# Contiguous decay rows, two wide operations on them, and modulation rows 2 to 5 formed on VectorE in the merge

## The chip, the cores and the metric

The kernel runs on one core of a Trainium2 chip. The metric is the device time of one execution in microseconds. The core has TensorE (PE, with a separate view for its weight loads, PEld), VectorE (DVE), ScalarE (ACT), GpSimd (POOL) and SyncE (SP); SP issues nearly all DMAs, in its program's order.

## The reference, cut to what matters

One layer: a token mixer with three branches (S5, Mamba-2, gated linear recurrence) that are merged by gates, then an expert-choice MoE. Both halves are modulated by six rows of 1024 values, `sc @ w_mod + b_mod`. Rows 0 and 1 are needed at the start; rows 2 to 5 only behind the merge. In the Mamba-2 branch the 1024 positions are cut in 8 chunks of 128. In a chunk each of 16 heads has a 128x128 matrix of decays, the exponential of a difference of running sums, for the forward and for the backward direction.

```python
def _mamba2_branch(z, xbc, dt_raw, p, h0):
    ...
    for d in range(2):
        dtd = dtv[:, :, d]
        xs, la, bs, cs = xm * dtd[..., None], dtd * a[d], bm, cm
        if d == 1:
            xs, la, bs, cs = _rev(xs), _rev(la), _rev(bs), _rev(cs)
        yd, fin = _ssd_scan(xs, la, bs, cs, None if h0 is None else h0[d])
        y = y + (yd if d == 0 else _rev(yd))

def _ssd_scan(xs, la, bm, cm, h0):           # chunks of 128 steps
    ...
    cb = jnp.einsum('bcqgn,bcsgn->bgcqs', cm, bm)
    lmat = jnp.exp(_segsum(a))
    y_diag = jnp.einsum('bgjcqs,bcsgjp->bcqgjp', cb[:, :, None] * lmat, xs)
    ...
    decay_out = jnp.exp(a_cum).transpose(0, 3, 4, 1, 2)
    y_off = jnp.einsum('bcqgn,bcgjpn->bcqgjp', cm, entering) * decay_out[..., None]

def _token_mixer(h, p, h0, rows):
    ...
    merged = g[:, :, 0] * ya + g[:, :, 1] * yb + g[:, :, 2] * yc
    return merged @ p['w_o'], (sa, sb, sc)

mod_x = jnp.split((sc @ w_mod[i] + b_mod[i])[:, None, :], 6, axis=-1)
mx, _ = _token_mixer(_modulate(x, norm1_g[i], mod_x[0], mod_x[1]), p, ctx_states, rows)
x = x + mod_x[2] * mx
x = x + mod_x[5] * _expert_choice_moe(_modulate(x, norm2_g[i], mod_x[3], mod_x[4]), p)
```

## The kernel before, in words

Everything is float32; large products are split in a high and a low part and made of three matmuls (L265, L266, L267). The stages follow one another in the span: modulation rows 0 and 1 and the norm; the projections and S5 (to about 530 us); the Mamba-2 stage, called p2 in the code (to 1131); the first half of the merge (1131 to 1270), its second half (to 1355), the output projection and router (to 1535), the experts.

In p2 the rows of running sums `XA` are transposed and stored to the DRAM tile `rowsd` by two DMAs (L731). `states()` then runs 9 steps in which POOL forms `xd` (L750), PE the state sums `st` (L752) and DVE scales the running state (`Sn`, L756). `chunk(g, c)` follows for 4 groups of heads and 8 chunks. It loads `xe`, `bc` and `rowb`: the last is 2 directions x 4 heads x 128 values, the same on all 128 partitions (L793), with three buffers. ACT forms `dec` from it (L796). DVE takes a column of `XL` off each of the 8 pieces of 128x128 and takes the smaller of that and `lim` (L801). ACT takes the exponential of all (L802), POOL adds the two directions (L803), DVE multiplies by `pcb` (L804), the product B times C from PE (L798). POOL multiplies `dec` by C (L805). PE then forms `yps` from `rowb` and `dec` (L814, L815). Every fourth chunk, `xq` is finished and stored to `m2_dram`.

Between the chunks stand other tasks: `z_task` (pj_z), the recurrence `lru_tile` (lps, lr, li, lq), `gate_task` (24 projections, pj_gt, ACT evacuates them as `gz` at L779) and `mod_task`, which for each half of modulation rows 2 to 5 loads 16 pieces `wm` of 128x1024 (two buffers, L909) and multiplies each on PE with a single column `scc`, so that the sums over 8 pieces stand in one bank `pm` (L912). Then the bias row `mr` is loaded, added (L917) and stored to `modd` (L918).

Nothing here is ordered by hand: a scheduler sets the order of each engine and of SP by its own estimate of times, and the pools decide which buffer is waited for. Evacuations have a higher priority. The output projection and the experts are ordered by hand and are not touched.

In the first half of the merge a loop over 8 output tiles d takes a load of weights (`raw_s`, split in `whi_s` and `wlo_s`, L972 and L973), and for each half of 512 positions three products of 12 matmuls: bog, bov and bol. ACT and DVE evacuate them (L1029 to L1033) into `mgs`, stored to `mgd`. At the end of a tile `load_y` loads one tile of `m2_dram` as `yr_m`, scales it (L985) and splits it in the pair `ym[d]` (L993, L994) for the second half of the merge. Modulation row 2 is read behind the merge, the others later.

## Time and profile before

| | us |
|---|---|
| median of three runs | 2121.89 (2120.39 to 2122.43) |
| the profiled execution | 2120.92 |
| its span in the trace | 2119.1 |
| PE busy | 1919.3 |
| DVE busy | 1525.2 |
| ACT busy | 1020.3 |
| POOL busy | 510.4 |

The span is what the trace shows of the profiled execution; 1.8 us lie around it. Busy times are of the whole span and mix stages with different limits. Matmuls overlap in the pipeline, so the durations of single matmuls add up to more than PE's busy time. PEclk is the share of full speed that TensorE's clock was granted.

### The profile page before, as it was taken

What the parts mean: (1) busy time and instruction counts of PE and PEld (TensorE: products, weight loads), DVE (VectorE), ACT (ScalarE), POOL (GpSimd) and SP (SyncE); (2) the same over time, 40 slices, a digit from 0 to 9 for tenths busy, and PEclk for the clock granted to TensorE, in tenths of its full rate; (3) what the DMA queues carried; (4) which work ended last, traced back from release to release, by engine and by line L of the source; (5) the groups of instructions that cost most, each with busy time, mean ns of one, the idle gap of its engine ahead of it and who ended that gap; (6) DMA issues with size and microseconds to landing.
All of it is one profiled execution on the core that took longest, in us unless ns stands there. A gap on an engine that the chain in (4) does not pass through costs nothing.

```text
span 2119.1 us, 27213 instructions
## 1 busy us (share of the span) xinstructions
PE 1919.3 (91%) x9630; PEld 1516.2 (72%) x9630; DVE 1525.2 (72%) x2232; ACT 1020.3 (48%) x1313; POOL 510.4 (24%) x489
## 2 busy tenths in 40 slices
PE   5989999988889988879999999898299999999997
PEld 2678888877657666456577888687188888888885
DVE  4787788783454777667434655628899999999998
ACT  4434434432213665446332212222188888888785
POOL 1353333330142344233100000234501111100122
PEclk9999999999999999989999999999599999999999
DMA  8234334422586676777666554554599999999983
GB/s 313 54 81 114 101 95 117 122 90 90 180 261 192 186 212 175 242 180 210 208 174 188 180 160 153 186 200 149 196 339 381 400 389 404 387 389 393 391 312 137
DMA packets 301554, 462.67 MB, mean 218 GB/s; under 512 B 39945, under 2 KB 200121, under 8 KB 300393
## 3 DMA queue, kind: packets, MB, share of 16 engines
q1 hardware_dynamic: 297096, 445.19, 62.2%
q0 software_dynamic: 4320, 15.73, 2.9%
q8 instruction: 76, 1.25, 0.2%
q14 instruction: 62, 0.50, 0.1%
HBM read 384.44 MB, written 78.51 MB: 218 GB/s over the span
## 4 chain that ended last, share of the span: by engine, by line
PE 55%; DMA 9%; DVE 7%; issue 2%; ACT 1%; SPq 1%; POOL 1%; DVEq 0%; ACTq 0%; POOLq 0%
PE h_w L1443 6%; PE h_w L1445 6%; PE h_w L1444 6%; PE wo L1268 3%; DMA rowb<-rowsd 3%; PE py_w L1445 3%; PE py_w L1443 3%; PE py_w L1444 3%; PE pj_gt L267 2%; PE pj_gt L265 2%; PE pj_gt L266 2%; DMA wm<-in_w_mod_dram 2%; PE bom L266 1%; PE bom L265 1%; PE st L752 1%
## 5 line engine op out<-in xcount | busy, mean ns | idle before, releaser
L1338 DVE TENSOR_TENSOR el_w<-er_w,eh_w 128x1024 fp32r<-128x1024 f32 x384 | 460.7, 1220 | 25.0 <-ACT eh_w L1337 11.1
L1337 ACT CAST eh_w<-er_w 128x1024 fp32r<-128x1024 f32 x384 | 403.7, 1052 | 135.4 <-PE h_w L1444 58.9
L1443 PE MATMUL h_w<-eh_w,thi_x 128*128 128x512 f32 x512 | 202.9, 396 | 0.0
L1445 PE MATMUL h_w<-el_w,thi_x 128*128 128x512 f32 x512 | 200.2, 391 | 0.0
L1444 PE MATMUL h_w<-eh_w,tlo_x 128*128 128x512 f32 x512 | 199.8, 390 | 0.0
L801 DVE SCALAR_TENSOR_TENSOR rowb<-rowb,XL,lim 128x128 f32<-128x128 f32 x256 | 116.1, 518 | 72.1 <-ACT dec L796 72.1
L265 PE MATMUL pj_gt<-hxh,whi_gt 128*128 128x512 f32 x384 | 155.9, 406 | 11.9 <-ACT gz L779 11.9
L267 PE MATMUL pj_gt<-hxh,wlo_gt 128*128 128x512 f32 x384 | 155.3, 404 | 0.0
L266 PE MATMUL pj_gt<-hxl,whi_gt 128*128 128x512 f32 x384 | 155.1, 404 | 0.0
L1445 PEld LDWEIGHTS h_w<-el_w,thi_x 128*128 128x128 f32 x512 | 96.2, 188 | 20.4
L1444 PEld LDWEIGHTS h_w<-eh_w,tlo_x 128*128 128x128 f32 x512 | 96.5, 188 | 19.6 <-DVE tlo_x L1362 0.4
L1443 PEld LDWEIGHTS h_w<-eh_w,thi_x 128*128 128x128 f32 x512 | 96.5, 188 | 19.2 <-ACT thi_x L1361 0.2
L265 PEld LDWEIGHTS pj_gt<-hxh,whi_gt 128*128 128x128 f32 x384 | 74.4, 194 | 38.0 <-ACT gz L779 16.1
L1346 POOL DMA_INDIRECT xs<-h2d,idx x16 | 23.3, 1459 | 309.5 <-PE tb_x L1354 294.4
L1443 PE MATMUL py_w<-eh_w,thi_h 128*128 128x512 f32 x240 | 96.3, 401 | 0.0
L1445 PE MATMUL py_w<-el_w,thi_h 128*128 128x512 f32 x240 | 94.0, 392 | 0.0
L1444 PE MATMUL py_w<-eh_w,tlo_h 128*128 128x512 f32 x240 | 93.5, 390 | 0.0
L267 PEld LDWEIGHTS pj_gt<-hxh,wlo_gt 128*128 128x128 f32 x384 | 74.4, 194 | 25.4 <-issue 9.6
L266 PEld LDWEIGHTS pj_gt<-hxl,whi_gt 128*128 128x128 f32 x384 | 74.4, 194 | 20.5 <-issue 4.9
L796 ACT ACTIVATE dec<-rowb 64x512 f32<-64x512 f32 x64 | 40.2, 629 | 82.7 <-DMA rowb<-rowsd 72.7
L267 PE MATMUL pj_xb<-hxh,wlo_xb 128*128 128x512 f32 x192 | 76.8, 400 | 0.5 <-DVE wlo_xb L128 0.5
L265 PE MATMUL pj_xb<-hxh,whi_xb 128*128 128x512 f32 x192 | 76.7, 399 | 0.0
(653 smaller groups left out, 4894.7 us busy)
## 6 DMA issues: line engine op xcount, KB each, us to landing
er_w<-in_moe_w_dram SPq DMA_DIRECT2D x384, 512.0 KB
wm<-in_w_mod_dram SPq DMA_DIRECT2D x32, 512.0 KB
rowb<-rowsd SPq DMA_DIRECT2D x32, 512.0 KB
raw_gt<-in_w_in_dram SPq DMA_DIRECT2D x24, 512.0 KB
gtd<-gz SPq DMA_DIRECT2D x48, 256.0 KB
xk<-xed SPq DMA_DIRECT2D x18, 512.0 KB
wm<-in_w_mod_dram SPq DMA_DIRECT2D x8, 1024.0 KB
xe<-xed SPq DMA_DIRECT2D x32, 256.0 KB
```

What stands on the lines that cost most here:

```text
L265: T.matmul(ps, wh(k), xh(k), start=(first and k == 0), stop=False)
L266: T.matmul(ps, wh(k), xl(k), start=False, stop=False)
L267: T.matmul(ps, wl(k), xh(k), start=False, stop=(last and k == nk - 1))
L796: A.activation(dec[64 * d:64 * d + 64], rowb[64 * d:64 * d + 64, d], AF.Exp)
L801: V.scalar_tensor_tensor(rowb[:, d, h], rowb[:, d, h], XL[:, c, d, 4 * g + h:4 * g + h + 1], lim[:, d], op0=ALU.subtract, op1=ALU.min)
L1268: T.matmul(st4[i]["ps"][n], ms[i][a][:, k], wo[k][b][:, sl], start=(k == 0 and q == 0), stop=(k == KC - 1 and q == 2))
L1337: A.copy(a, raw)
L1338: V.tensor_sub(b, raw, a.bitcast(F32))
L1346: G.indirect_dma_start(out=xsb[e], out_offset=None, in_=h2d[:, :], in_offset=bass.IndirectOffsetOnAxis(ap=idx[:, e:e + 1], axis=0))
L1443: T.matmul(ps[n], xa[:, j, :], a[:, sl], start=(j == 0), stop=False)
L1444: T.matmul(ps[n], xb[:, j, :], a[:, sl], start=False, stop=False)
L1445: T.matmul(ps[n], xa[:, j, :], b[:, sl], start=False, stop=(j == KC - 1))
```

## The change

Three things. (1) `rowsd` is laid out by group, chunk, direction, head and position. The stores become eight DMAs instead of two, and the load of `rowb` takes one run of 4 KB for each partition, where it was eight runs of 512 bytes. (2) The eight small DVE operations of a chunk become two over 128x1024 with broadcast operands: a subtraction (L801 after) and a minimum (L802). The sum of the two directions is on DVE (L804) instead of POOL. (3) `mod_task` is gone from p2. `mod_part(q, j)` loads one piece `wm` in the first half of the merge and multiplies it on DVE by `scc`, as a value for each partition, adding to the sum of row q (L1001 for the first piece, L1003 for the seven others). When 8 pieces are summed, two matmuls with a column of ones add the partitions (L1008). 5, 5, 5, 5, 4, 4, 4 and 0 pieces follow the store of output tiles 0 to 7. The pieces share 16 buffers with the pairs `ym[d]`, which are now taken one tile at a time.

```diff
--- before.py
+++ after.py
@@ -676,7 +676,7 @@
     lru_dram = dr.tile([4, P, S], F32, name="lru_dram")
     modd = dr.tile([4, D], F32, name="modd")
     m2_dram = [dr.tile([P, 2, S], F32, name=f"m2_dram{g}") for g in range(4)]
-    rowsd = dr.tile([4, 2, 4, S], F32, name="rowsd")
+    rowsd = dr.tile([4, 8, 2, 4, P], F32, name="rowsd")
     rbd = dr.tile([1, S], F32, name="rbd")
     gtd = [[dr.tile([P, S], F32, name=f"gtd{b}{d}") for d in range(KC)] for b in range(3)]
     zp = hstack.enter_context(tc.tile_pool(name="zp", bufs=1, reuse_waits="tile"))
@@ -728,7 +728,8 @@
                 T.transpose(pr_[0:32, q * P:(q + 1) * P], XA[:, 4 * h + q].rearrange("p d h -> p (d h)"), ident)
             V.tensor_copy(rw[:, h * 512:(h + 1) * 512], pr_[0:32, :])
         for d in range(2):
-            Y.dma_start(dap(rowsd, d * 4 * S, [[8 * S, 4], [S, 4], [1, S]]), rw[16 * d:16 * d + 16])
+            for g in range(4):
+                Y.dma_start(dap(rowsd, g * 8 * S + d * 512, [[P, 4], [8 * P, 8], [1, P]]), rw[16 * d + 4 * g:16 * d + 4 * g + 4].rearrange("h (c q) -> h c q", c=8))
         Dc = p2.tile([P, 8], F32, name="Dc")
         for hh in range(2):
             Y.dma_start(Dc[64 * hh:64 * hh + 64, :], dap(I["m2_d"], hh, [[0, 64], [2, 8]]))
@@ -790,17 +791,17 @@
             Y.dma_start(bc_, bcd[g][:, :, q0:q0 + P])
             Bc, Cd = bc_[0:64, 0, :], bc_[:, 1, :]
             rowb = p2.tile([P, 2, 4, P], F32, tag="rowb", name=f"rowb{g}{c}", bufs=3)
-            Y.dma_start(rowb.rearrange("p d h q -> p (d h) q"), dap(rowsd, g * 8 * S + q0, [[0, P], [S, 8], [1, P]]))
+            Y.dma_start(rowb.rearrange("p d h q -> p (d h q)"), dap(rowsd, (8 * g + c) * 8 * P, [[0, P], [1, 8 * P]]))
             dec = p2.tile([P, 4, P], F32, tag="dec", name=f"dec{g}{c}", bufs=2)
             for d in range(2):
                 A.activation(dec[64 * d:64 * d + 64], rowb[64 * d:64 * d + 64, d], AF.Exp)
             pcb = bank(f"pcb{g}{c}")
             T.matmul(pcb[:, 0:P], Bc, Cd[0:64, :], start=True, stop=True)
-            for d in range(2):
-                for h in range(4):
-                    V.scalar_tensor_tensor(rowb[:, d, h], rowb[:, d, h], XL[:, c, d, 4 * g + h:4 * g + h + 1], lim[:, d], op0=ALU.subtract, op1=ALU.min)
+            sh = [P, 2, 4, P]
+            V.tensor_sub(rowb, rowb, XL[:, c, :, 4 * g:4 * g + 4][:, :, :, None].to_broadcast(sh))
+            V.tensor_tensor(rowb, rowb, lim[:, :, None, :].to_broadcast(sh), op=ALU.min)
             A.activation(rowb, rowb, AF.Exp)
-            G.tensor_add(rowb[:, 0], rowb[:, 0], rowb[:, 1])
+            V.tensor_add(rowb[:, 0], rowb[:, 0], rowb[:, 1])
             V.tensor_mul(rowb[:, 0], rowb[:, 0], pcb[:, None, 0:P].to_broadcast([P, 4, P]))
             G.tensor_mul(dec, dec, Cd[:, None, :].to_broadcast([P, 4, P]))
             if c % 4 == 0:
@@ -900,23 +901,6 @@
                     Y.dma_start(lru_dram[t], hs)
                 yield
 
-
-        def mod_task(half):
-            pm = psp.tile([P, 512], F32, tag="pm", name=f"pm2_{half}", bufs=1)
-            for j in range(KC):
-                for q in range(2):
-                    wm = p2.tile([P, 1024], F32, tag="wm2", name=f"wm{half}{j}{q}", bufs=2)
-                    Y.dma_start(wm, dap(I["w_mod"], j * 6 * D + 2 * D + half * 2 * D + q * D, [[KC * 6 * D, P], [1, 1024]]))
-                    for n in range(2):
-                        r = 32 * (2 * q + n)
-                        T.matmul(pm[r:r + 1, :], scc[:, j, 0:1], wm[:, n * 512:(n + 1) * 512], start=(j == 0), stop=(j == KC - 1))
-            for n in range(4):
-                mr = p2.tile([P, 512], F32, tag="mr", name=f"mr{half}{n}", bufs=1)
-                r = slice(32 * n, 32 * n + 1)
-                Y.dma_start(mr[r], dap(I["b_mod"], 2 * D + half * 2 * D + n * 512, [[1, 1], [1, 512]]))
-                V.tensor_add(mr[r], mr[r], pm[r, :])
-                Y.dma_start(dap(modd, half * 2 * D + n * 512, [[1, 1], [1, 512]]), mr[r])
-
         zs = [lambda t=t: z_task(t) for t in range(2, 8)]
         lrus = (s_ for t in range(4) for s_ in lru_tile(t))
         for g in range(4):
@@ -940,8 +924,6 @@
         for b in range(3):
             for d in range(KC):
                 gate_task(b, d)
-            if b < 2:
-                mod_task(b)
     if dbg is not None:
         [emit(f"m2{g}", m2_dram[g]) for g in range(4)]; emit("rbc", rbd)
     if stop == "p2":
@@ -973,7 +955,7 @@
                 V.tensor_sub(lo[:, 0:n], raw[:, 0:n], hi[:, 0:n].bitcast(F32))
             return hi, lo
 
-        ym = [(p3b.tile([P, S], F32R, name=f"yhi_m{k}"), p3b.tile([P, S], F32R, name=f"ylo_m{k}")) for k in range(8)]
+        ym = []
         rbc = p3b.tile([P, S], F32, name="rbc3")
         m2h = p3b.tile([P, 8], F32, name="m2h")
         V.tensor_scalar(m2h, pcols[:, PC["m2g"]:PC["m2g"] + 8], 0.5, None, op0=ALU.mult)
@@ -1006,6 +988,30 @@
         gt0.append(gtile("gtf"))
         sg0.append(half("sgf"))
         wl0 = [p3b.tile([P, 12, P], F32R, tag="wlo", name="wlo_f", bufs=2)]
+
+
+        mq = {}
+        mparts = [(q, j) for q in range(4) for j in range(KC)]
+
+        def mod_part(q, j):
+            wm = p3b.tile([P, D], F32, tag="ym", name=f"wm{q}{j}", bufs=16)
+            Y.dma_start(wm, dap(I["w_mod"], j * 6 * D + 2 * D + q * D, [[KC * 6 * D, P], [1, D]]))
+            if j == 0:
+                mq[q] = wm
+                V.tensor_scalar(wm, wm, scc[:, j, 0:1], None, op0=ALU.mult)
+                return
+            V.scalar_tensor_tensor(mq[q], wm, scc[:, j, 0:1], mq[q], op0=ALU.mult, op1=ALU.add)
+            if j < KC - 1:
+                return
+            pm = psp.tile([P, 512], F32, tag="pm", name=f"pm2_{q}", bufs=1)
+            for n in range(2):
+                T.matmul(pm[32 * n:32 * n + 1, :], ones[:, 0:1], mq[q][:, n * 512:(n + 1) * 512], start=True, stop=True)
+            for n in range(2):
+                r = slice(32 * n, 32 * n + 1)
+                mr = p3b.tile([P, 512], F32, tag="mr", name=f"mr{q}{n}", bufs=1)
+                Y.dma_start(mr[r], dap(I["b_mod"], 2 * D + q * D + n * 512, [[1, 1], [1, 512]]))
+                V.tensor_add(mr[r], mr[r], pm[r, :])
+                Y.dma_start(dap(modd, q * D + n * 512, [[1, 1], [1, 512]]), mr[r])
 
         if True:
             yp_ = lambda nm: (mst("yhi_" + nm), mst("ylo_" + nm))
@@ -1032,6 +1038,9 @@
                         V.scalar_tensor_tensor(s3, gt[:, 1], 1.0, pl_, op0=ALU.add, op1=ALU.mult)
                         V.scalar_tensor_tensor(mg[:, sl], s2, 0.5, s3, op0=ALU.mult, op1=ALU.add)
                 Y.dma_start(mgd[d], mg)
+                for _ in range((5, 5, 5, 5, 4, 4, 4, 0)[d]):
+                    mod_part(*mparts.pop(0))
+                ym.append(tuple(p3b.tile([P, S], F32R, tag="ym", name=f"y{e}_m{d}", bufs=16) for e in ("hi", "lo")))
                 load_y(ym[d], m2_dram[d // 2][:, d % 2, :], f"m{d}", m2h[:, d:d + 1])
 
         wr = bp.tile([P, KC, 16], F32, name="wr")
```

The scheduler sets the new order. DVE among the chunks: `rowb` with a number is the tile of one chunk, `wlo_gt` the low part of gate weights, `l..` tiles of the recurrence. Before:

```order
L801 SCALAR_TENSOR_TENSOR rowb_5365<-rowb_5365,XL,lim 128x128 x8
L804 TENSOR_TENSOR rowb_5319<-rowb_5319,pcb_5324 128x512
L885 SCALAR_TENSOR_TENSOR lq_5393<-lq_5393,lr_5296 128x1283
L804 TENSOR_TENSOR rowb_5365<-rowb_5365,pcb_5370 128x512
L801 SCALAR_TENSOR_TENSOR rowb_5411<-rowb_5411,XL,lim 128x128 x8
L887 SCALAR_TENSOR_TENSOR li_5297<-li_5297,lxc_4965 128x1283
L128 TENSOR_TENSOR wlo_gt_7150<-raw_gt_7147,whi_gt_7149 128x1024
L888 SCALAR_TENSOR_TENSOR li_5297<-lq_5393,li_5297 128x1283
L804 TENSOR_TENSOR rowb_5411<-rowb_5411,pcb_5416 128x512
L801 SCALAR_TENSOR_TENSOR rowb_5454<-rowb_5454,XL,lim 128x128 x4
```

The next chunk is prepared beside the products of the one before. After, at the same place:

```order
L801 TENSOR_TENSOR rowb_5375<-rowb_5375,XL 128x1024
L888 SCALAR_TENSOR_TENSOR li_5273<-li_5273,lxc_4965 128x1283
L802 TENSOR_TENSOR rowb_5375<-rowb_5375,lim 128x1024
L889 SCALAR_TENSOR_TENSOR li_5273<-lq_5357,li_5273 128x1283
L895 SCALAR_TENSOR_TENSOR lq_5357<-la_5356,li_5273 128x256
L804 TENSOR_TENSOR rowb_5375<-rowb_5375 128x512
L896 SCALAR_TENSOR_TENSOR lq_5357<-la_5356,lq_5357,li_5273 128x1024
L805 TENSOR_TENSOR rowb_5375<-rowb_5375,pcb_5380 128x512
L801 TENSOR_TENSOR rowb_5412<-rowb_5412,XL 128x1024
L897 TENSOR_TENSOR lh_5179<-lh_5179,lq_5357 128x1024
L802 TENSOR_TENSOR rowb_5412<-rowb_5412,lim 128x1024
```

A row of eight small operations is two wide ones, with other work between them, and the addition L804 stands on DVE ahead of the product, now L805.

PE among the chunks, before; `pm_1` is the bank of the second pair of modulation rows:

```order
L267 MATMUL pj_gt_512_7944<-hxh_372,wlo_gt_7913 128x512
L265 MATMUL pj_gt_512_7944<-hxh_373,whi_gt_7912 128x512
L266 MATMUL pj_gt_512_7944<-hxl_381,whi_gt_7912 128x512
L267 MATMUL pj_gt_512_7944<-hxh_373,wlo_gt_7913 128x512
L912 MATMUL pm_1_7972<-wm_7985,scc 1x512 x2
L912 MATMUL pm_1_7972<-wm_7989,scc 1x512 x2
L265 MATMUL pj_gt_0_8059<-hxh_366,whi_gt_8055 128x512
L266 MATMUL pj_gt_0_8059<-hxl_374,whi_gt_8055 128x512
L267 MATMUL pj_gt_0_8059<-hxh_366,wlo_gt_8056 128x512
```

Two pieces `wm` are multiplied in a row between gate matmuls. PE in output tile 2 of the merge, after; `ones` is the column that adds the partitions:

```order
L267 MATMUL bog_8563<-yhi_s_8245,wlo_s_8552 128x512
L265 MATMUL bog_8563<-yhi_s_8251,whi_s_8550 128x512
L266 MATMUL bog_8563<-ylo_s_8252,whi_s_8550 128x512
L267 MATMUL bog_8563<-yhi_s_8251,wlo_s_8552 128x512
L1008 MATMUL pm_0_8526<-wm_8387,ones 1x512 x2
L265 MATMUL bov_8562<-yhi_s_8233,whi_s_8550 128x512
L266 MATMUL bov_8562<-ylo_s_8234,whi_s_8550 128x512
L267 MATMUL bov_8562<-yhi_s_8233,wlo_s_8552 128x512
```

All 64 modulation matmuls are gone from the chunk stage and the tail of gates; eight stand in the merge, between two products of a tile. Behind the last yps 347 gate matmuls stood before, and 278 stand there now.

DVE in the merge, one output tile, before; `s` are the evacuations of bog, bov and bol:

```order
L1030 SCALAR_TENSOR_TENSOR s_8920<-s_8920,bov_8881 128x512
L1031 SCALAR_TENSOR_TENSOR s_8920<-gt_8878,s_8920 128x512
L1032 SCALAR_TENSOR_TENSOR s_8921<-gt_8878,bol_8883 128x512
L1033 SCALAR_TENSOR_TENSOR mgs_8877<-s_8920,s_8921 128x512
L985 SCALAR_TENSOR_TENSOR yr_m_8977<-yr_m_8977,m2h,rbc_8591 128x1024
L1030 SCALAR_TENSOR_TENSOR s_8969<-s_8969,bov_8930 128x512
L1031 SCALAR_TENSOR_TENSOR s_8969<-gt_8927,s_8969 128x512
L994 TENSOR_TENSOR ylo_m_8580<-yr_m_8977,yhi_m_8579 128x1024
L1032 SCALAR_TENSOR_TENSOR s_8970<-gt_8927,bol_8932 128x512
L1033 SCALAR_TENSOR_TENSOR mgs_8877<-s_8969,s_8970 128x512
L973 TENSOR_TENSOR wlo_s_9097<-raw_s_9096,whi_s_9095 128x1536
```

The evacuations of a tile have only one wide step of `load_y` among them and the split of the next weights. After, the second tile; `wm_8387` is the sum of the first row, `wm_8537` that of the next:

```order
L1038 SCALAR_TENSOR_TENSOR s_8461<-gt_8418,bol_8423 128x512
L1039 SCALAR_TENSOR_TENSOR mgs_8417<-s_8460,s_8461 128x512
L1003 SCALAR_TENSOR_TENSOR wm_8387<-wm_8517,scc,wm_8387 128x1024
L1003 SCALAR_TENSOR_TENSOR wm_8387<-wm_8520,scc,wm_8387 128x1024
L1003 SCALAR_TENSOR_TENSOR wm_8387<-wm_8523,scc,wm_8387 128x1024
L1036 SCALAR_TENSOR_TENSOR s_8509<-s_8509,bov_8470 128x512
L1001 TENSOR_SCALAR wm_8537<-wm_8537,scc 128x1024
L1037 SCALAR_TENSOR_TENSOR s_8509<-gt_8467,s_8509 128x512
L1003 SCALAR_TENSOR_TENSOR wm_8537<-wm_8540,scc,wm_8537 128x1024
L1038 SCALAR_TENSOR_TENSOR s_8510<-gt_8467,bol_8472 128x512
L955 TENSOR_TENSOR wlo_s_8682<-raw_s_8681,whi_s_8680 128x1536
L967 SCALAR_TENSOR_TENSOR yr_m_8545<-yr_m_8545,m2h,rbc_8227 128x1024
```

Five multiplications with `wm` are between the evacuations of one tile, each behind its own load. On SP the five loads stand behind the store of `mgd` of the tile before and ahead of the load of `yr_m`. From the end of the merge's first half on, the order of every engine is that of before.

## Rows read from the trace of the kernel before

**Rows 1.** The page, busy us, share and instructions of each engine.
```profile
PE 1919.3 (91%) x9630; PEld 1516.2 (72%) x9630; DVE 1525.2 (72%) x2232; ACT 1020.3 (48%) x1313; POOL 510.4 (24%) x489
```

**Rows 2.** Stretches of the span: PE, PEld, DVE, ACT, POOL busy (instructions), PEclk, DMA share, GB/s.
```profile
560.00:690.00 130.00, 120.56 (x524) 81.67 (x523) 56.36 (x76) 30.54 (x39) 46.94 (x28) 0.96 0.72 219
690.00:1050.00 360.00, 305.79 (x1586) 218.18 (x1583) 249.84 (x361) 193.82 (x250) 127.58 (x96) 0.92 0.72 203
1050.00:1131.00 81.00, 78.62 (x345) 60.38 (x344) 27.05 (x32) 27.84 (x29) 1.66 (x1) 1.00 0.56 163
1131.00:1270.00 139.00, 139.00 (x597) 111.65 (x596) 76.43 (x92) 28.28 (x32) 0.00 (x0) 1.00 0.57 180
```

**Rows 3.** The same for line L912 alone: PE and PEld busy, PEclk, DMA share, GB/s.
```profile
1050.00:1131.00 81.00, 4.11 (x16) 0.37 (x16) 1.00 0.56 163
sum 571.00, PE 31.92 PEld 2.71; mean PE 10.64 PEld 0.90
```

**Rows 4.** Waits of PE, 560 to 1131: total us, times, longest.
```profile
PE pm L912 <- DMA wm<-in_w_mod_dram: 15.7, 4, 5.9
PE yps L814 <- DVE rowb L804: 14.8, 5, 3.5
PE pj_gt L265 <- ACT gz L779: 11.9, 8, 4.8
PE st L752 <- POOL xd L750: 9.4, 1, 9.4
```

**Rows 5.** The chain of 690 to 1050: shares by line, then pieces: start, us, what.
```profile
by line: DMA rowb<-rowsd 17.1%; DMA wm<-in_w_mod_dram 9.8%; DVE rowb L801 7.1%; PE pj_gt L266 6.9%; PE pj_gt L267 6.9%; PE pj_gt L265 6.7%; issue 5.4%; DMA m_dram<-xq 5.4%; PE pm L912 5.1%; PE lps L878 4.7%; DMA mr<-in_b_mod_dram 3.6%; PE y
...
690.90 8.95 DMA rowb<-rowsd
...
767.12 11.44 DMA rowb<-rowsd
...
843.32 8.80 DMA wm<-in_w_mod_dram
852.16 1.87 PE pm L912 x4
```

**Rows 6.** Waits of all engines, 560 to 1131.
```profile
POOL dec L805 <- ACT dec L796: 109.6, 21, 11.4
ACT dec L796 <- DMA rowb<-rowsd: 72.7, 14, 14.6
DVE rowb L801 <- ACT dec L796: 72.1, 18, 14.6
POOL rowb L803 <- ACT rowb L802: 52.8, 20, 6.1
```

**Rows 7.** Waits of SP's queue, 690 to 1050.
```profile
SPq L909 <- PE pm L912: 25.7, 11, 5.2
...
SPq L918 <- DVE mr L917: 6.7, 3, 4.3
```

**Rows 8.** Groups of instructions, 560 to 1131: busy us, mean ns, idle before, releasers.
```profile
L801 DVE SCALAR_TENSOR_TENSOR rowb<-rowb,XL,lim 128x128 f32<-128x128 f32 x256 | 116.1, 518 | 72.1 <-ACT dec L796 72.1
...
L803 POOL TENSOR_TENSOR rowb<-rowb 128x512 f32<-128x512 f32 x32 | 42.5, 1330 | 56.8 <-ACT rowb L802 52.8 <-DMA gtd<-gz 4.0
...
L804 DVE TENSOR_TENSOR rowb<-rowb,pcb 128x512 f32<-128x512 f32 x32 | 21.7, 677 | 18.8 <-PE pcb L798 13.4 <-POOL rowb L803 5.3
...
L825 DVE TENSOR_TENSOR xq<-xq,zq 128x512 f32<-128x512 f32 x16 | 13.3, 834 | 0.0
```

**Rows 9.** Timeline of DVE: L756 beside an operation of POOL, and alone.
```profile
616.76 2.47 DVE L756 TENSOR_TENSOR Sn<-Sn,decS 128x1024 f32<-128x1024 f32 x1
...
636.01 1.23 DVE L756 TENSOR_TENSOR Sn<-Sn,decS 128x1024 f32<-128x1024 f32 x1
```

**Rows 10.** DMA queue 1: packets, MB, share; 690 to 1050, then 1600 to 2000.
```profile
q1 hardware_dynamic: 74741, 72.92, 71.3%
```
```profile
q1 hardware_dynamic: 39656, 144.42, 90.1%
```

**Rows 11.** One output tile of the merge's first half, and the mean of six.
```profile
1155.40:1172.40 17.00, 17.00 (x74) 13.66 (x74) 9.28 (x12) 3.52 (x4) 0.00 (x0) 1.00 0.52 176
...
sum 100.80, PE 100.80 PEld 81.03 DVE 55.74 ACT 21.46 POOL 0.00; mean PE 16.80 PEld 13.50 DVE 9.29 ACT 3.58 POOL 0.00
```

**Rows 12.** DVE groups, 1131 to 1270.
```profile
L985 DVE SCALAR_TENSOR_TENSOR yr_m<-yr_m,m2h,rbc 128x1024 f32<-128x1024 f32 x8 | 10.3, 1284 | 41.2 <-DMA yr_m<-m_dram 41.2
```

## The prediction

> **What bounds the kernel now.** I read the busy totals first, then the stages, then the waits of the stages that the change touches, then the chain. TensorE (PE) is busy for 1919.3 us of 2119.1 [rows 1], so a saving counts only where it takes work from PE, or an idle stretch in which PE waits. The stage table [rows 2] shows where such stretches are: in the state and chunk stages and the tail of gates (560 to 1131) PE is busy 120.56, 305.79 and 78.62 us, together 504.97 of 571, so 66.0 idle, of which 54.2 lie in the chunk stage (690 to 1050); there the granted clock is 0.92. The first half of the merge (1131 to 1270) is PE without a gap. The 66 us by their releasers [rows 4]: 15.7 for a modulation load wm, 14.8 for rowb from DVE L804, 11.9 for the gate evacuation, 9.4 for POOL's xd, the rest small.
>
> The chain of the chunk stage [rows 5] says which work ended last. Its shares: rowb's load 17.1%, wm's load 9.8%, the small DVE operations L801 7.1%, the modulation's matmuls 5.1%, its bias rows 3.6%. Its pieces alternate between a rowb landing (8.95, 11.44 us) and wm landings (8.80 us) with 1.87 us of matmuls behind. So two things set this stage: the chunk's own path (rowb, L796, L801, L802, L803, L804, yps) and the modulation work put into it. The waits of all engines agree [rows 6]: ScalarE waits 72.7 us for rowb, POOL 109.6 and DVE 72.1 for ScalarE behind it. And on SP's queue [rows 7] 25.7 us pass at the wm issue waiting for PE to free one of two wm buffers, 6.7 at the modd store; every rowb load behind them is late by that.
>
> **Part 1, modulation out of the chunk stage.** PE loses the matmuls of L912: 31.92 us in the three stretches [rows 3]. PE work leaves whole where PE sets the end, as in the tail, so I take 31.9. The wait for wm goes with it: 15.7. The chain prices the same removal independently: 9.8 + 5.1 + 3.6 = 18.5% of 360 = 66.6 us for everything that the modulation holds there, bias rows too. The sum 47.6 is inside that.
>
> **Part 2, the rowb path.** What is left of PE's idle time is 66.0 − 15.7 = 50.3, or 50.3 − 9.4 = 40.9 without the xd wait, which the change does not touch. All of it hangs on chunk operations (rowb, gates' and LRU's evacuations) that run behind late loads. Three things shorten that path: rowb lands sooner, SP's queue is rid of 32 wm and 16 row DMAs and of the 32.4 us blocked at them, and the sum of both halves no longer crosses to POOL (L803, 1.33 us each and its wait, [rows 6, 8]). Against that, the gates filling PE between chunks keep their own waits. I take half, 20.4; the ends are 0 and 40.9.
>
> How much sooner rowb lands: in 690 to 1050 queue 1 moves 74741 packets of 976 bytes on average in 71.3% of 16 engines' time, 55 ns each; in a stretch of the expert stage 39656 of 3642 bytes in 90.1%, 145 ns [rows 10]. A line through both is 22 ns + 0.034 ns a byte, an estimate: 39 ns for a 512-byte piece, 160 ns for 4 KB. The load of 512 KB is then 1024 × 39 / 16 = 2.5 us of the 16 engines before and 128 × 160 / 16 = 1.3 after. In the chunk stage 28 such loads save 34 us and the 24 wm loads that leave take 31 with them, so the DMA share falls from 0.72 to about 0.54 for the same length. The Trainium skill ("DMA: Bandwidth & Descriptors", Specifications) puts the smallest transfer at line rate at 512 B; by that the longer run would save no transfer time, and the sum would be that of rival 2, below. The trace's two points speak against it.
>
> **Part 3, DVE in the chunks.** Removed: 256 L801 operations, 116.1 us [rows 8]. Added: 64 of 128x1024 with a broadcast operand; the nearest row is L756 (broadcast, same shape): 1.23 us alone and 2.47 beside POOL [rows 9], mean 1.70; so 64 × 1.23 to 1.70 = 79 to 109 us. Also 32 additions of 128x512, by L804's 0.68 to L825's 0.83: 22 to 27 us. Together 101 to 136 against 116.1: neutral on DVE, and the same on the path (per chunk some 3.2 us for eight small ones before, 2.5 to 3.4 for two wide ones). I count 0, ends −15 and +20. These rows show that a wide DVE operation takes twice its time beside POOL. The Trainium skill ("SBUF — State Buffer", SBUF: two separate sides) tells that as an exclusive lock for a whole instruction between a DVE operation with two SBUF inputs and a GpSimd one; the trace agrees with 1.23 against 2.47.
>
> **Part 4, the stores of rowsd.** Six more DMAs ahead of the first chunk. No row has one issue alone; SP's time for the chunks' DMAs lies under the states. I take 2 us, ends 0 and 5.
>
> **Part 5, the merge's first half.** PE gains 8 one-row matmuls, which the profile counts as 16 (L912's 64 in the code are 128 in the profile); in the tail 16 such take 4.11 us [rows 3]: 4.1. DVE: a tile of 16.8 us holds 9.29 us of DVE work [rows 11]; five wide multiply-adds at 1.284, the price of L985 with the same shape [rows 12], add 6.4, and a row pair at 0.68 each in every second tile 0.7 on average: 16.4 in the first four tiles, 15.1 in the next three. No POOL work lies there, so the price alone holds. It fits by 0.4 us. DMA: share 0.57 of 16.8 is 9.6, and five loads at 1.3 make it 16.1, also just full. The order on DVE puts the multiply-adds, each behind its own load, between the evacuations s of bov and bol; behind a late load wait the evacuation, then the bank, then PE. Also SP is in order: the weights raw_s of a coming tile are behind wm loads that wait for mgd's evacuation. So the cover is thin. Low end 0. High end: one wait for a transfer as DVE has it now, 41.2 / 8 = 5.15 us [rows 12], in each of seven tiles: 36. I take 7.8: the four five-part tiles run over by one wide operation and one row, 1.28 + 0.68 each. The later rows of modd are read behind this half, at its end, and the order from there on is unchanged: 0.
>
> **Sum.** −31.9 − 15.7 − 20.4 + 0 + 2 + 4.1 + 7.8 = −54.1 on the profiled 2120.92: 2066.8. That run is 0.97 below the median of the runs; predicted 2067 us.
>
> **Rivals.**
> 1. *More of the chunk stage comes back.* The path no longer binds PE: all 40.9 and half of the clock's loss, 0.5 × 0.08 × 305.8 = 12. That is −31.9 − 15.7 − 40.9 − 12 + 2 + 4.1 + 0 = −94: 2027. For it: gates as filler. Against: gates have their own waits, 11.9 us [rows 4]. Chance 0.16.
> 2. *The chunk path stays as long as it is*, since rowb's landing is set by when a buffer comes free and not by its length, or since the wide operations keep POOL's dec product waiting (1.23 instead of 0.34 us, 32 times, 28 us). Then the last yps stays in its place, and the gain is the shorter tail: 347 gate matmuls stand behind it before and 278 now, 69 × 0.23 us (17.00 us for 74, [rows 11]) = 15.9, and the tail's pm 4.1, with the wm waits' 15.7: −36 + 2 + 11.9 = −22: 2099. The rule on 512 bytes that the Trainium skill ("DMA: Bandwidth & Descriptors", Specifications) states would give this one. Chance 0.18.
> 3. *The merge is bound by DVE and DMA*, at the high end: −68 + 2 + 4.1 + 36 = −26: 2095. Chance 0.10.
> 4. *Slower: multiply-adds queued ahead of evacuations stall PE for a whole wm landing per tile.* Place: DVE in seven tiles. Price: 8.8 to 11 us, as wm and rowb landings take in the chunk stage [rows 5], 7 times: 62 to 77. From 62 / 7 = 8.9 us a tile it eats the gain: 2121 to 2136. Against: the loads stand half a tile to a tile ahead of their use, and the DMA there is at 0.52 to 0.60. Chance 0.06.
> 5. *Nothing*, the gains and costs cancel within 4 us: 0.03.
>
> My forecast has what is left, 0.47, with its own range 2045 to 2088. The range of all reaches from rival 1 to rivals 2 and 3, a little past both: 2026 to 2104; it leaves out rivals 4 and 5 and some of rival 1, about 0.17. Faster by over 0.2% (4.2 us, about what a measurement here tells from no change): 0.47 + 0.16 + 0.18 + 0.10 = 0.91. Slower: 0.06. Within: 0.03.
>
> **What would show it.** Part 1: no pm matmuls and no wm landings on the chain between 690 and the merge. Part 2: ScalarE's wait for rowb well under 72.7 us, and the merge starting about 66 us sooner (near 1065); if it starts near 1097, rival 2. Part 3: 128x1024 operations of 1.2 to 1.7 us mean at L801 and L802. Part 5: first half 139 + 12; a PE gap before bog or bov with a releaser s or wlo_s is rival 3, and one of 9 us a tile rival 4. I am wrong in the mechanism if the stages behind the merge change by over 5 us.

## The result, and the profile after

The changed kernel takes 2041.93 us (median of four runs, 2040.74 to 2045.45) against 2122.14 for the kernel before: a ratio of 0.9626, with a 95% interval of 0.961 to 0.9643. That is 80 us less; the prediction was 2067, so 55 less, with a range down to 2026. The profiled execution took 2041.05 us, its span is 2039.3. One of the four executions of the kernel with late ends, below, took 6084 us at a granted clock of 0.31 and stands outside its comparison.

To see where the 80 us lie, both traces are cut at the same work: first and last state matmul `st`, last `yps`, first `bol`, first `bom`. The first four stretches are the states, the chunks, the tail of gates, and the merge's first half. Columns as in [rows 2]. Before:

```profile
565.90:664.60 98.70, 89.27 (x370) 57.92 (x370) 44.05 (x56) 15.57 (x21) 38.00 (x22) 0.95 0.74 229
664.60:1036.70 372.10, 317.89 (x1649) 229.89 (x1649) 253.19 (x371) 205.35 (x261) 129.36 (x98) 0.93 0.70 198
1036.70:1130.20 93.50, 91.12 (x401) 67.09 (x398) 32.38 (x38) 30.24 (x33) 5.05 (x3) 1.00 0.60 180
1130.20:1263.70 133.50, 133.50 (x573) 107.23 (x573) 73.37 (x87) 27.67 (x32) 0.00 (x0) 1.00 0.57 179
```

After:

```profile
562.00:646.20 84.20, 84.20 (x352) 55.92 (x352) 48.82 (x46) 15.56 (x21) 38.36 (x20) 1.00 0.75 237
646.20:967.80 321.60, 300.27 (x1640) 234.90 (x1640) 256.75 (x217) 207.59 (x266) 112.92 (x68) 0.98 0.63 199
967.80:1038.90 71.10, 66.76 (x301) 53.93 (x299) 26.82 (x23) 25.89 (x27) 4.24 (x3) 1.00 0.56 171
1038.90:1184.50 145.60, 139.88 (x590) 107.82 (x590) 114.58 (x135) 27.18 (x31) 0.00 (x0) 0.99 0.83 282
```

The states take 14.5 us less, the chunks 50.5 and the tail 22.4; the merge's first half takes 12.1 more. The states start 3.9 us sooner, which is no part of the change: PE's order up to there is that of before, and over the kernels below that start lies anywhere from 561.2 to 566.7. From the first bom to the first expert matmul both kernels take the same, 272.7 and 272.3 us (1263.7 to 1536.4, 1184.5 to 1456.8).

In states, chunks and tail PE is idle for 66.0 of 564.3 us before and 25.7 of 476.9 after: 40.3 back. PE's busy time there falls from 498.28 to 451.23, by 47.1; the modulation's matmuls explain 31.9, and the other 15.1 go with the granted clock, which was 0.95 and 0.93 and is now 1.00 and 0.98. The page's engine row, which answers [rows 1], and PE's waits from 540 to 1300, which answer [rows 4]:

```profile
PE 1878.4 (92%) x9518; PEld 1506.5 (74%) x9518; DVE 1570.4 (77%) x2104; ACT 1018.7 (50%) x1313; POOL 495.3 (24%) x457
```

```profile
PE pj_gt L265 <- ACT gz L780: 9.1, 6, 3.3
PE yps L815 <- DVE rowb L805: 6.7, 3, 3.4
PE pj_z L265 <- DVE zt L773: 6.7, 1, 6.7
...
PE yps L815 <- issue: 5.3, 3, 3.3
PE pm L1008 <- DVE wm L1003: 5.2, 2, 3.1
```

The waits for wm (15.7 us) and for POOL's xd (9.4) are gone; yps waits 6.7 us for DVE, where it waited 14.8. All engines, as in [rows 6], and the chunk's operations, as in [rows 8]:

```profile
ACT rowb L803 <- DVE rowb L802: 61.0, 17, 6.9
...
DVE rowb L801 <- ACT dec L797: 36.3, 14, 4.4
...
ACT dec L797 <- DMA rowb<-rowsd: 24.5, 8, 9.2
```

```profile
L806 POOL TENSOR_TENSOR dec<-dec,bc 128x512 f32<-128x512 f32 x32 | 65.1, 2035 | 92.3 <-ACT dec L797 78.7 <-DMA raw_gt<-in_w_in_dram 6.0 <-DMA rowb<-rowsd 3.8
L802 DVE TENSOR_TENSOR rowb<-rowb,lim 128x1024 f32<-128x1024 f32 x32 | 57.4, 1793 | 0.6
L801 DVE TENSOR_TENSOR rowb<-rowb,XL 128x1024 f32<-128x1024 f32 x32 | 48.1, 1502 | 36.3 <-ACT dec L797 36.3
...
L804 DVE TENSOR_TENSOR rowb<-rowb 128x512 f32<-128x512 f32 x32 | 26.0, 816 | 6.0 <-ACT rowb L803 6.0
```

ScalarE waits 24.5 us for rowb, a third of the 72.7 of before. ScalarE's longest wait is now for the second wide operation (61.0). The two wide operations take 48.1 + 57.4 = 105.5 us where the eight small ones took 116.1. POOL's product with C (L806) takes 2.04 us each where it took 1.46.

The merge's first half, DVE and PE groups, and its DMA queue:

```profile
L1003 DVE SCALAR_TENSOR_TENSOR wm<-wm,scc,wm 128x1024 f32<-128x1024 f32 x28 | 35.9, 1282 | 12.2 <-DMA wm<-in_w_mod_dram 12.1
...
L1001 DVE TENSOR_SCALAR wm<-wm,scc 128x1024 f32<-128x1024 f32 x4 | 3.0, 752 | 6.4 <-DMA wm<-in_w_mod_dram 6.4
```

```profile
L1008 PE MATMUL pm<-wm,ones 128*1 128x512 f32 x16 | 5.0, 702 | 5.2 <-DVE wm L1003 5.2
```

```profile
q1 hardware_dynamic: 26569, 40.80, 82.7%
```

A multiply-add costs 1.282 us, as L985 did [rows 12]. The first piece of a row, a single-source operation, takes 0.752. DVE waits 12.1 + 6.4 us for wm loads, PE 5.2 us for DVE at the matmuls that end a row, and these take 5.0 us. The DMA share is 0.83, where 0.57 was.

### The profile page after: what moved, and what is told of

Its sections match the earlier page's. It is cut to its first block, busy times and chain, and to the rows that moved or that the text cites. A ratio compares the mean times of both kernels' runs of the same rounds, so it can differ in the third digit from the quotient of the medians.

```text
span 2039.3 us, 26816 instructions
## 1 busy us (share of the span) xinstructions
PE 1878.4 (92%) x9518; PEld 1506.5 (74%) x9518; DVE 1570.4 (77%) x2104; ACT 1018.7 (50%) x1313; POOL 495.3 (24%) x457
## 4 chain that ended last, share of the span: by engine, by line
PE 42%; DVE 6%; DMA 2%; issue 1%; POOL 1%; SPq 0%; ACT 0%; DVEq 0%; ACTq 0%
PE h_w L1452 6%; PE h_w L1454 6%; PE h_w L1453 6%; PE wo L1277 3%; PE py_w L1454 3%; PE py_w L1452 3%; PE py_w L1453 3%; PE bom L266 1%; PE bom L265 1%; PE bom L267 1%; DVE tu L1118 1%; DMA wm<-in_w_mod_dram 1%; PE tb_x L1363 1%; PE tb_h L1363 1%; DVE tv L1115 1%
## 5 line engine op out<-in xcount | busy, mean ns | idle before, releaser
L1454 PEld LDWEIGHTS h_w<-el_w,thi_x 128*128 128x128 f32 x512 | 96.2, 188 | 20.4
L806 POOL TENSOR_TENSOR dec<-dec,bc 128x512 f32<-128x512 f32 x32 | 65.1, 2035 | 92.3 <-ACT dec L797 78.7
L267 PEld LDWEIGHTS pj_gt<-hxh,wlo_gt 128*128 128x128 f32 x384 | 72.7, 189 | 15.8 <-issue 0.2
L266 PE MATMUL pj_xb<-hxl,whi_xb 128*128 128x512 f32 x192 | 76.7, 399 | 0.0
```

Of the source, the lines that this page charges most:

```text
L266: T.matmul(ps, wh(k), xl(k), start=False, stop=False)
L267: T.matmul(ps, wl(k), xh(k), start=False, stop=(last and k == nk - 1))
L806: G.tensor_mul(dec, dec, Cd[:, None, :].to_broadcast([P, 4, P]))
L1454: T.matmul(ps[n], xa[:, j, :], b[:, sl], start=False, stop=(j == KC - 1))
```

## The experiments

The first kernels do one part alone; later ones undo one part of the changed kernel. The kernel before was timed again beside each of the four groups of experiments, with medians of 2117.1 to 2120.5; each ratio is to the median of its own group, and a few us between kernels of different groups are no difference. Of each edit only the lines that matter are shown. Since a scheduler sets the order, an edit moves instructions far from it; where two kernels have the same order, the text says so.

**Modulation alone.**

```diff
 # rowsd, rowb load, L801, L803 as before
-            if b < 2:
-                mod_task(b)
+                for _ in range((5, 5, 5, 5, 4, 4, 4, 0)[d]):
+                    mod_part(*mparts.pop(0))
```

> Only the modulation rows move to the merge; rows of decays, the eight small operations and POOL's addition stay as before. Theory (the modulation work is the larger part, and takes its share of idle time and clock with it): 2122 - 31.9 - 15.7 - half of the 40.3 us idle that came back beyond wm - half of the clock's 15 + 12 in the merge, about 2065 to 2075, with the merge's first half at 145 us. Rival (most of what came back beyond the matmuls hangs on the rowb path): 2122 - 47.6 + 12 = 2086 or more, ScalarE still waiting over 60 us for rowb.

Measured 2099.15, against 2117.05 before: ratio 0.9913 (0.9885 to 0.9941), 18 us. The theory falls: the part that was to bring most brings less than a quarter, and ScalarE still waits 63.5 us for rowb. In states, chunks and tail PE is idle for 61.8 us, where it was idle for 66.0: the wait for wm is gone, but others have grown in its place, for the gates' evacuation (16.0, before 11.9), for the recurrence's lr (11.0, before 6.9) and for rowb (17.4, before 14.8). So little more than the matmuls themselves came back, and the merge took a part of that.

**The chunk stage alone.**

```diff
 # mod_task stays among the chunks; the rest as in the change
-        rowsd = dr.tile([4, 2, 4, S], ...)
+        rowsd = dr.tile([4, 8, 2, 4, P], ...)
-                    V.scalar_tensor_tensor(...)      # eight
+            V.tensor_sub(...); V.tensor_tensor(...)  # two
-            G.tensor_add(...)
+            V.tensor_add(...)
```

> Contiguous rows, two wide operations and the addition on DVE; the modulation stays on PE among the chunks. Theory: the rest, 15 to 25 us faster than before, 2097 to 2107, the merge's first half at 133.5 as before. Rival (the rowb path is what mattered): 40 us or more faster, at or under 2082.

Measured 2059.84, ratio 0.9734 (0.9707 to 0.976): 57 us. The rival holds.

**The layout alone.** The shape of `rowsd` changes as in the change; the stores and the load are:

```diff
-            Y.dma_start(dap(rowsd, d * 4 * S, [[8 * S, 4], [S, 4], [1, S]]), rw[16 * d:16 * d + 16])
+            for g in range(4):
+                Y.dma_start(dap(rowsd, g * 8 * S + d * 512, [[P, 4], [8 * P, 8], [1, P]]), ...)
-            Y.dma_start(rowb, dap(rowsd, g * 8 * S + q0, [[0, P], [S, 8], [1, P]]))
+            Y.dma_start(rowb, dap(rowsd, (8 * g + c) * 8 * P, [[0, P], [1, 8 * P]]))
```

> Only the layout of the decay rows; everything else as before. Theory (4 KB runs halve the transfer of 32 loads, which is a part of the path): 5 to 15 us faster, ScalarE's wait for rowb from 72.7 to 40 to 55 us. Rival (the landing is set by buffers and SP's queue, not by its length): within 4 us of before, and the wait stays above 65 us.

Measured 2068.87, ratio 0.9773 (0.9746 to 0.98): 48 us, far more than the theory gave, and the wait of ScalarE for rowb is 18.9 us. PE's waits of this kernel, which still has all modulation matmuls and loads among its chunks, are the surprise:

```profile
PE yps L815 <- DVE rowb L805: 15.3, 7, 3.8
PE pj_z L265 <- DVE zt L773: 6.2, 1, 6.2
PE pj_gt L265 <- ACT gz L780: 6.2, 4, 2.8
PE pcb L799 <- ACT li L880: 1.5, 1, 1.5
PE bog L267 <- DVE wlo_f L974: 1.2, 1, 1.2
```

The wait for wm of [rows 4] does not show at all, with all of the modulation's loads still there: it was no price of these loads by themselves. The wait for xd is gone too, and the clock is back:

```profile
565.50:654.30 88.80, 88.80 (x376) 57.31 (x376) 47.33 (x56) 15.67 (x21) 36.98 (x22) 1.00 0.83 265
654.30:980.60 326.30, 304.08 (x1632) 224.91 (x1632) 255.42 (x372) 204.56 (x261) 132.88 (x98) 0.96 0.68 219
980.60:1076.40 95.80, 94.94 (x410) 68.18 (x407) 30.50 (x37) 29.72 (x32) 4.26 (x3) 1.00 0.61 192
```

PE busy is 88.80 + 304.08 + 94.94 = 487.8 us here, 10.5 less than before, with the same matmuls; that difference goes with the clock. PE's idle time in the three stages is 23.1 us, where it was 66.0.

**What in the layout counts: order, length or place.** The layout changes three things: the scheduler's order (two stores become eight), the length of the runs, and the distance of the runs in DRAM. Three kernels have on every engine, SP too, exactly the order of the layout alone and differ only in the store and load of the rows. The first keeps the old layout:

```diff
-            Y.dma_start(dap(rowsd, d * 4 * S, [[8 * S, 4], [S, 4], [1, S]]), rw[16 * d:16 * d + 16])
+            for g in range(4):
+                Y.dma_start(dap(rowsd, g * 8 * S + d * 4 * S, [[S, 4], [1, S]]), rw[16 * d + 4 * g:16 * d + 4 * g + 4])
```

> The kernel before with one edit: the decay rows are stored to the old layout by eight DMAs instead of two. Every engine's order is then that of the kernel with the layout alone, but the loads still fetch eight runs of 512 bytes. Theory (the 48 us of the layout alone come from the loads themselves, 4 KB runs): no more than 10 us faster than before, at or above 2107, ScalarE waiting over 60 us for rowb. Rival (they come from the order that the scheduler found around eight stores): 35 to 50 us faster, 2067 to 2082.

Measured 2109.52 against 2117.88, ratio 0.9961 (0.9947 to 0.9975). The order is worth 8 us; the loads are the rest. About half of the wait for wm goes with the order, and the clock of the chunks stays at 0.93:

```profile
PE pm L913 <- DMA wm<-in_w_mod_dram: 7.6, 3, 3.7
```

```profile
660.20:1020.90 360.70, 314.99 (x1632) 231.65 (x1632) 251.31 (x372) 205.51 (x261) 128.93 (x98) 0.93 0.70 198
```

The second has the new layout but loads it in pieces of 512 bytes (the edit against the layout alone):

```diff
-            rowb = p2.tile([P, 2, 4, P], F32, ...)
+            rowb = p2.tile([P, 2, 4, P + 1], F32, ...)[:, :, :, 0:P]
-            Y.dma_start(rowb, dap(rowsd, (8 * g + c) * 8 * P, [[0, P], [1, 8 * P]]))
+            Y.dma_start(rowb, dap(rowsd, (8 * g + c) * 8 * P, [[0, P], [P, 8], [1, P]]))
```

> The layout alone again, but rowb is padded by one value between its rows, so that each load falls into pieces of 512 bytes, read from 4 KB that lie together in DRAM; the order is that of the layout alone. Theory (the number of pieces counts): as the old loads in the same order, at least 25 us slower than the layout alone, 2094 or more. Rival (that the rows lie together in DRAM counts): within 8 us of the layout alone, 2061 to 2077. If the order counts, this one and the one with eight stores both lie near 2069.

Measured 2066.79, ratio 0.9756 (0.9737 to 0.9774): as fast as the runs of 4 KB (2068.87). The number of pieces is worth nothing here. From 690 to 940 the kernel with the 4 KB runs moves the same bytes in fewer packets:

```profile
q1 hardware_dynamic: 41097, 57.44, 70.4%
```

The kernel with pieces moves 62587 in 73.6% (below), so a further packet costs some 6 ns of one engine. Between the kernel with pieces and the first of the three the order, the number and the size of the pieces are the same; what differs is the distance between the eight rows in DRAM, 4096 bytes in the first, 512 in the second, and the pad in `rowb`. The chain between 690 and 940, the rowb landings, first with 4096, then with 512:

```profile
686.49 8.89 DMA rowb<-rowsd
...
770.77 12.70 DMA rowb<-rowsd
...
794.31 9.83 DMA rowb<-rowsd
...
929.85 10.17 DMA rowb<-rowsd
```

```profile
751.71 7.34 DMA rowb<-rowsd
...
779.15 5.10 DMA rowb<-rowsd
...
927.82 6.33 DMA rowb<-rowsd
```

ScalarE's wait for rowb, and queue 1 in the same stretch, in the same order:

```profile
ACT dec L797 <- DMA rowb<-rowsd: 58.9, 16, 14.6
```

```profile
q1 hardware_dynamic: 54012, 49.58, 71.7%
```

```profile
ACT dec L797 <- DMA rowb<-rowsd: 17.8, 4, 10.1
```

```profile
q1 hardware_dynamic: 62587, 57.43, 73.6%
```

The packets are of the same mean size (918 bytes), but 54012 take 71.7% of the engines' 250 us and 62587 take 73.6%: 53 ns each against 47, for all packets together, of which rowb's are a part only. In the packet records of this stretch a packet of 512 bytes takes 27 ns at the median in both kernels, but 5.4% of them take over 100 ns with the rows 4096 bytes apart and 0.6% with 512: most are as fast, and some are held up.

The third keeps the old layout and its pieces, and pads the row in DRAM (the edit against the first of the three):

```diff
-    rowsd = dr.tile([4, 2, 4, S], F32, name="rowsd")
+    rowsd = dr.tile([4, 2, 4, S + P], F32, name="rowsd")   # and S + P for S in store and load
```

> As the kernel with eight stores to the old layout (same order on every engine, loads of eight runs of 512 bytes), but a row of decays takes 1152 values in DRAM instead of 1024, so that the eight runs of a load lie 4608 bytes apart instead of 4096. Theory (128 partitions reading runs that lie exactly 4096 bytes apart are slow; a pitch off that is not): like the contiguous rows in pieces, 2060 to 2080, rowb landings on the chain of 5 to 7.5 us. Rival (what counts is that the 4 KB lie together, at whatever pitch otherwise): like the eight stores alone, 2100 to 2115, landings of 9 to 12 us.

Measured 2069.07, ratio 0.976 (0.9733 to 0.9787). The rows now lie 4608 bytes apart, further than before, and the load is as fast as with contiguous rows. So neither closeness nor length counts: of the three distances tried, 512, 4096 and 4608 bytes, the one of exactly 4096 was slow. Only 0.5% of the packets of 512 bytes take over 100 ns. The landings on the chain, and what is left of the wait for wm:

```profile
751.64 6.98 DMA rowb<-rowsd
...
778.70 5.25 DMA rowb<-rowsd
```

```profile
PE pm L913 <- DMA wm<-in_w_mod_dram: 1.4, 1, 1.4
```

In one and the same order the wait for wm is thus 7.6 us with 4096 bytes, 1.4 with 4608 and none with 512. That the slow loads of rowb delay those of wm fits this; no run isolates it.

**The changed kernel with the old loads.** The order on every engine is that of the changed kernel; layout and loads are the old ones, with eight stores.

```diff
-            Y.dma_start(rowb, dap(rowsd, (8 * g + c) * 8 * P, [[0, P], [1, 8 * P]]))
+            Y.dma_start(rowb, dap(rowsd, g * 8 * S + q0, [[0, P], [S, 8], [1, P]]))
```

> The changed kernel in its own order, but with the old layout of the decay rows and loads of eight runs of 512 bytes. Theory (4 KB runs are worth what the layout alone showed): 30 to 50 us slower than the changed kernel, 2072 to 2092. Rival (with the modulation gone from the chunk stage the DMAs have room, and the runs are worth little): within 12 us, 2042 to 2054.

Measured 2102.27, 60 us slower than the changed kernel's 2041.93; ratio to the kernel before 0.9923 (0.9897 to 0.9949). Room on the DMA queues does not replace the layout: ScalarE's wait for rowb is 81.2 us in it.

**The price in the merge.** One kernel leaves out the modulation's sums and 28 of its 32 loads, so its modulation rows are not those of the reference:

```diff
         def mod_part(q, j):
+            if j < KC - 1:
+                return
             wm = ...   # and its load
-            V.scalar_tensor_tensor(mq[q], wm, scc[:, j, 0:1], mq[q], op0=ALU.mult, op1=ALU.add)
+            mq[q] = wm
```

> The changed kernel without 28 of the 32 modulation loads and without all of their multiply-adds (each row's last piece goes to the two matmuls as it is), so the modulation rows 2 to 5 are not those of the reference. Theory (the merge's 12 us are the modulation's: 5.0 matmuls, 5.7 PE gaps, the rest clock): the matmuls stay, the gaps go, so 5 to 8 us faster than the changed kernel, 2034 to 2037, the first half of the merge at 138 to 141. Rival (the gaps come from PE's own order, not from DVE and DMA): the same as the changed kernel within 2 us.

Measured 2034.98 (2031.55 to 2038.99), 7 us below the changed kernel. The ratios to the kernel before, 0.9606 (0.9585 to 0.9627) and 0.9626 (0.961 to 0.9643), overlap, so the time alone does not tell them apart; the stretch of the merge below does. Another puts the end of a row one tile later:

```diff
+                for q in late:          # rows finished by the tile before
+                    mod_row(q)          # two matmuls, bias, store
                 for _ in range((5, 5, 5, 5, 4, 4, 4, 0)[d]):
                     mod_part(*mparts.pop(0))
```

> The changed kernel with the two matmuls that end a modulation row, and its bias row, put one output tile later in the code, so that PE meets them half a tile to a tile after the last multiply-add. Theory (the merge lost 5.2 us to PE waiting at pm for DVE): 4 to 5 us faster than the changed kernel, about 2037, the merge's first half at about 140. Rival (the wait only moves to the evacuations behind full DVE and DMA): within 1.5 us of the changed kernel, 2041 to 2043.

Measured 2040.36 (2039.73 to 2040.39 but for the execution named above), 1.6 us below the changed kernel, which is no difference that these runs can tell. The first half of the merge, from the first bol to the first bom, without the sums, then with late ends:

```profile
1042.00:1180.30 138.30, 137.81 (x588) 106.95 (x587) 79.83 (x104) 26.96 (x31) 0.00 (x0) 1.00 0.59 192
```

```profile
1043.10:1181.70 138.60, 138.11 (x589) 107.22 (x587) 112.52 (x133) 26.83 (x31) 0.00 (x0) 1.00 0.84 294
```

Without the sums and their loads the gap goes and the matmuls stay, as the theory said; 138.3 us against the changed kernel's 145.6. Late ends take PE's gap away too (138.11 busy of 138.60), 7 us less in this stretch than the changed kernel. But its span is only 0.7 less: the first bol comes 4.2 us later (1043.1 against 1038.9), 2.9 of which is the start of the states, and from the first bom to the last are 91.0 us (1181.7 to 1272.7) against 88.9. So the median's 1.6 fits the rival; where the rest of these 7 us goes is not shown.

**The operations of the chunk.** The changed kernel with eight small operations:

```diff
-            V.tensor_sub(rowb, rowb, XL[...].to_broadcast(sh))
-            V.tensor_tensor(rowb, rowb, lim[...].to_broadcast(sh), op=ALU.min)
+            for d in range(2):
+                for h in range(4):
+                    V.scalar_tensor_tensor(rowb[:, d, h], ..., op0=ALU.subtract, op1=ALU.min)
```

> The changed kernel with the eight small operations in place of the two wide ones (the addition stays on DVE); the order around them moves with it. Theory (the wide operations cost as much as the small ones: 105.5 us measured against 116.1): within 8 us of the changed kernel, 2034 to 2050. Rival A (wide ones stand 2 us each beside POOL and hold its product with C): 10 us or more faster, under 2032. Rival B (the wide ones are what let the chunks be short): 10 us or more slower, over 2052.

Measured 2031.28, ratio 0.9588 (0.9567 to 0.9608): faster than both kernels, 10.7 us below the changed one (the interval of its ratio ends where that of the changed kernel begins, at 0.961). In it, the chunk's groups and PE's waits:

```profile
L802 DVE SCALAR_TENSOR_TENSOR rowb<-rowb,XL,lim 128x128 f32<-128x128 f32 x256 | 115.8, 518 | 14.1 <-ACT dec L797 14.0
...
L806 POOL TENSOR_TENSOR dec<-dec,bc 128x512 f32<-128x512 f32 x32 | 47.9, 1496 | 90.2 <-ACT dec L797 74.9 <-issue 5.1 <-DMA rowb<-rowsd 3.8
```

```profile
PE pj_gt L265 <- ACT gz L780: 8.7, 7, 2.2
...
PE yps L815 <- issue: 5.0, 2, 3.0
```

The small ones are 115.8 us in all, more than the wide ones, yet POOL's product takes 1.50 us beside them and 2.04 beside the wide ones, and PE does not wait for DVE at yps at all (6.7 us in the changed kernel). The order differs too, so how much is POOL's delay and how much order is not shown.

Then without both changes of operations:

```diff
+            # eight small operations, and
-            V.tensor_add(rowb[:, 0], rowb[:, 0], rowb[:, 1])
+            G.tensor_add(rowb[:, 0], rowb[:, 0], rowb[:, 1])
```

> The changed kernel without both of its changes to the chunk's operations: eight small operations, and the addition of the directions on POOL. Contiguous rows and the modulation in the merge stay. Theory (the two wide operations cost 10 us, and the addition on DVE is worth a few): between the version with small operations and the changed kernel, 2031 to 2042. Rival (a step over POOL on the chunk's path costs more): over 2045.

Measured 2057.35, ratio 0.9715 (0.9687 to 0.9744): 26 us slower than with the addition on DVE. The time is the rival's. PE's waits at yps and behind gates:

```profile
PE pj_gt L265 <- ACT gz L780: 11.1, 6, 3.1
PE yps L815 <- DVE rowb L805: 8.9, 6, 2.9
```

The step over POOL is not itself what comes late: from the end of the exponential to the end of the sum the median of the 32 chunks is 1.39 us on POOL and 1.45 on DVE. States, chunks and tail together, first with the addition on POOL, then on DVE:

```profile
sum 492.50, PE 461.95 PEld 349.72 DVE 325.41 ACT 249.27 POOL 174.38; mean PE 153.98 PEld 116.57 DVE 108.47 ACT 83.09 POOL 58.12
```

```profile
sum 465.20, PE 447.23 PEld 341.79 DVE 326.41 ACT 249.68 POOL 129.42; mean PE 149.08 PEld 113.93 DVE 108.80 ACT 83.23 POOL 43.14
```

Of the 27.3 us between them 12.6 are idle time of PE and 14.7 are busy time for the same matmuls, which goes with the granted clock (0.96 and 0.99 in the chunks). The order differs as well, and which of its changes makes PE idle is not shown.

The last one joins small operations and late ends:

```diff
 # eight small operations, mod_row(q) one tile later
```

> The version with small operations, and the two matmuls and the bias row of each modulation row one output tile later. Theory (both effects add, the later matmuls being worth 1 to 2 us by their own run): 2027 to 2031. Rival (the order that moves with it counts for more than that): outside 2025 to 2034.

Measured 2033.04 (2029.9 to 2033.96), ratio 0.9594 (0.9567 to 0.9621): the same as the small operations alone. The late ends bring nothing that lasts.

In a row of one part at a time the 80 us read: layout −48 (2117.1 to 2068.9), modulation −11.5 (to 2057.4), the addition on DVE −26 (to 2031.3), the wide operations +10.7 (to 2041.9); the rest is the scatter of the kernel before between the groups. Each step also moves the scheduler's order, and the order of the steps matters: the layout is worth 60 when it comes last.

## Why the prediction was right or wrong

The direction and the range were right, the size a third short (55 us of 80), and the cause was put in the wrong place. The time lies 3 us below the forecast's own range (2045 to 2088), between it and rival 1.

- **The sum by terms.** PE's matmuls: −31.9, as measured. Idle time: 15.7 + 20.4 = 36.1 forecast, 40.3 measured, which is luck: the modulation alone brought back 4.2 of it, and the layout alone 42.9. The clock: 0 in the sum and 12 in rival 1, 15.1 measured; this is the term that was mis-sized. The merge begins 91 us sooner (1038.9, before 1130.2), where 66 were forecast. The rowsd stores: +2 forecast, nothing to be seen. The merge: +11.9 forecast, 12.1 measured. With 3.9 of an early start that belongs to the run, −31.9 − 40.3 − 15.1 − 3.9 + 12.1 = −79.1, of 79.8 in the span.
- **Part 1, the wait for wm.** This step failed. The 15.7 us were put down to the modulation, and the chain's 18.5% were read as a second witness. Taking the modulation away alone brought 18 us with its own cost in the merge, and other waits took the place of the 15.7; changing the layout alone took the wait for wm away with the loads still there. A late landing on the chain names the load that was late, not the one that made it late.
- **Part 2, the rowb path.** The mechanism was rowb's load, but by another property. The estimate of 39 and 160 ns from two stretches of mixed traffic gave half the transfer by length, with 22 ns for a further packet. The two kernels with one layout show some 6. The runs in pieces cost the same as the 4 KB runs (2066.79 and 2068.87). So the rule of the Trainium skill ("DMA: Bandwidth & Descriptors", Specifications), by which 512 B are enough for line rate, agrees with the runs, and the prediction was wrong to hold the two points against it; what that rule does not say is that the pitch of the rows counted. The 9.4 us of xd, left out as untouched by the change, are gone with the layout alone as well (4.4 are left with the order alone).
- **Part 3, DVE neutral.** 131.5 us with the additions (48.1 + 57.4 + 26.0), inside the 101 to 136, though the second wide operation takes 1.79 us where 1.2 to 1.7 were named. But neutral DVE time is not neutral on the path: the wide operations cost 10.7 us, the addition on DVE brought 26. The wide operations had been counted at 0, and the addition stood without a price of its own among the three things behind Part 2's 20.4. That a wide operation beside POOL holds POOL was named in rival 2; in the trace POOL's product takes 2.29 us in the 22 chunks where a wide operation runs beside it and 1.47 in the other ten, and the wide operations take 1.21 us where POOL is idle. The trace fits the exclusion that the Trainium skill ("SBUF — State Buffer", SBUF: two separate sides) states; what it is worth on the path no run isolates.
- **Part 5, the merge.** Its size was right, 12.1 for 11.9: the multiply-adds cost 1.282 for 1.284 forecast and the matmuls 5.0 for 4.1. The place of the waits was not: evacuations were not late, PE waited at the two matmuls that end a row (5.2 us), and DVE's waits for wm, 18.5 us in all, fell in idle time but for what PE waited there.
- **Rivals.** Rival 1 (2027, more comes back) is nearest in size, since the clock came back. Rival 2 did not occur, but its picture is what the kernel shows with the old pitch: 2102.27 measured, 2099 forecast; the agreement is luck, since neither of its two reasons is the pitch. Rivals 3 and 4 did not occur.

What stays open: why a distance of 4096 bytes is slow, which other distances are, and whether loads that are not broadcast to 128 partitions are slow too; and how the 26 and 10.7 us of the operations divide between the operations and the order that moved with them.

## What to carry to other kernels

When many loads on the chain land late, look at the addresses of the one that is broadcast to all partitions, not only at its pieces' length; pad its pitch off 4096 bytes and measure before anything is restructured. To tell a transfer from a scheduler's order, make kernels whose order is the same and that differ in the transfer alone. Do not put a term at nothing because an engine's busy total stays the same: which engine takes a short addition, and whether the operations beside GpSimd are two wide ones or eight small ones, went here with 26 and 10.7 us, by themselves or by the order that they bring.
